# One mixer and the output projection of a diffusion block: where gates leave PSUM, which banks the decay loop uses, and when loads and read-backs are issued

## Chip, cores, metric

The kernel runs on one core of a Trainium2 chip, as one program in one launch. The metric is the device time of one execution in microseconds; a measurement is the median over several runs of the same kernel on the same chip. "PE" is TensorE, "PEld" its weight loads, "DVE" VectorE, "ACT" ScalarE, "POOL" GpSimd, "SP" the engine whose queue issues most of the transfers.

## The reference

One layer of a token mixer with three parallel head groups, a common output projection and an MLP, for 2048 latent and 256 context tokens, 1024 channels, in float32. Cut to what the change touches:

```python
(xa, ga, qb, kb, vb, gb, lr, qc, kc, vc, oc, i_fw, i_bw, f_fw, f_bw) = split_proj(h @ w_in)
# group B: gated linear attention in chunks of 64, 6 heads of 64, both directions d
la = heads(log_sigmoid(lr @ gla_w2[d] + gla_b2[d]) / 16)
b = cumsum(la, axis=chunk)            # decay inside a chunk
q_dec, k_dec = q * exp(b), k * exp(-b)
scores = where(causal, q_dec @ k_dec.T, 0)
u = (k * exp(b_last - b)).T @ v       # what a chunk adds to the state
s = exp(b_last) * s + u               # scan over the chunks, s_prev is s before
o = scores @ v + q_dec @ s_prev
# all groups
gate = concat(gelu(ga), silu(gb), sigmoid(oc))
y = head_rmsnorm(concat(yA, yB, yC), head_norm_g) * gate
x = x + g1 * (y @ w_out)
x = x + g2 * (relu(modulate(rmsnorm(x, norm2_g), sh2, sc2) @ w1) ** 2 @ w2)
return rmsnorm(x, final_g)
```

## The kernel before

The tokens lie in five groups (group 0 the 256 context tokens, groups 1 to 4 of 512 latent tokens). The stages follow each other in one long program: norm and modulation (to about 200 us), mixer A, the modulation of the MLP, mixer C (to about 800 us), mixer B (about 800 to 1250), the output projection (to 1480), the MLP (to the end).

Every matrix product of the projections is made of three float32 products with rounded operands, high by high, high by low and low by high (`products`, lines 357 to 371): for one block of 128 channels and one group that is 24 matmuls of 128x512 into one PSUM bank `acc`, after which `evac` takes the bank. Blocks of the input projection don't run in a stage of their own: `Filler` hands them out piecewise, so that they stand between the mixers' small matmuls. The order on PE is the order in which the program is written (a manual schedule). The other engines get their order from a scheduler, with priorities in a few places.

PSUM has eight banks here: three `pp` (block products), one `tr` (transposes, `trt`), and four of the mixer's own. In mixer B these four are one ring, `qk2`, from which the decay's pre-activation `xq`, the state products `u` and, in the second loop, the scores take their banks.

A gate block (`to_gate`, L489) turns a bank into GELU (blocks 0 and 1), SiLU (2 to 4) or sigmoid (5 to 7). It goes back and forth between ACT (square, absolute value, exponential, logarithm, exponential) and DVE (L497, L498 for GELU, L502 and L505), with the tile `t` and the bank itself as operands, and its bank is free only after the last product, L505. `evt` has three buffers.

Mixer B's first loop walks 30 steps (6 heads by 5 groups). `decay` loads the low-rank input on POOL's queue (`lr`, L1027), multiplies it into `xq`, computes log-sigmoid, the scan L1039 and the exponentials, and scales the keys `k` and queries `q`, which it stores. Three steps later `keys_t` transposes the keys into `trt()` and ACT copies them (`kt`, L1067). One step after that `chunk_u` multiplies them with the values into a bank `u`, and two DVE copies (L1077, L1079) take it to the state `U`; `chain` scans the state. Between these, `fil.share` runs gate blocks.

The second loop walks 24 steps (group, head pair, head). `scores` loads `q` and `k` (`qdD` and `kdD`, names `bk` and `bq`, four and three buffers) and pads `q` into `z` (L1147 on ACT, L1148 on DVE, three buffers), multiplies (L1155), and masks. `outputs`, two steps later, multiplies the scores with the values and the queries with the state (L1166, L1167). Between the two, `between_b` runs the remaining filler, then the loads of the output weights (`load_wo`), then the output projection as a generator, as far as the rows of y are ready.

The output projection works on 16 tiles of 128 tokens. `y_in` loads the gates `ga` and the mixers' output `yt`, squares it into `sq` (ACT, L1229), and scales it by its heads' norms (DVE, L1234). `y_t` transposes half a tile, multiplies it with the gates (L1249) and splits it into `yh` (ACT, L1250) and `yl` (POOL, L1251). `w_out` makes one half of 512 columns (24 matmuls, L1264 to L1266) and adds it to `x2` (DVE, L1269). `x_out` stores `x2`, normalises it into `xo` (L1278 squares it there, L1280 scales it) and stores that (L1281). Normalised tiles are read back (`xn`, L1343), transposed and modulated by `h2_tile` (L1312) for the first half of the MLP, among the products of later tiles. The pool of the projection has two `yt`, one `sq`, one `xo`, one `xn`.

## Time and profile before

| | |
|---|---|
| median of three runs | 2781.36 us (2778.57 to 2790.45) |
| the profiled execution | 2780.29 us, span 2778.5 us |
| PE busy | 2561.5 us, 92% of the span, 12239 instructions |
| PEld busy | 2081.4 us, 75% |
| DVE busy | 1754.9 us, 63% |
| ACT busy | 1161.4 us, 42% |
| POOL busy | 982.4 us, 35% |
| mean granted clock of PE | 0.965 |

Busy times are sums over one execution. An engine's idle time in a stretch is the stretch's length less its busy time there; the profile names for most of it the instruction that ended it. Register, branch, semaphore and DMA-issuing instructions don't count as busy. All lines are those of the kernel before.

### The profile page before, as it was taken

What the parts mean: (1) busy time and instruction counts of PE and PEld (TensorE: products, weight loads), DVE (VectorE), ACT (ScalarE), POOL (GpSimd) and SP (SyncE); (2) the same over time, 40 slices, a digit from 0 to 9 for tenths busy, and PEclk for the clock granted to TensorE, in tenths of its full rate; (3) what the DMA queues carried; (4) which work ended last, traced back from release to release, by engine and by line L of the source; (5) the groups of instructions that cost most, each with busy time, mean ns of one, the idle gap of its engine ahead of it and who ended that gap; (6) DMA issues with size and microseconds to landing.
All of it is one profiled execution on the core that took longest, in us unless ns stands there. A gap on an engine that the chain in (4) does not pass through costs nothing. (4 is left out here: it accounts for less than half of the span.)

```text
span 2778.5 us, 36372 instructions
## 1 busy us (share of the span) xinstructions
PE 2561.5 (92%) x12239; PEld 2081.4 (75%) x12239; DVE 1754.9 (63%) x3039; ACT 1161.4 (42%) x2053; POOL 982.4 (35%) x868
## 2 busy tenths in 40 slices
PE   5798889899999888888897999989999999999997
PEld 3676667788887676777776888867887888888876
DVE  7855476146646986656665787666666356545586
ACT  6755521133335666433334444544445332222343
POOL 5734411245444443334443343343432122222221
PEclk8999989999999999989998999999999999999999
DMA  7443355565656666766663777555554677656564
GB/s 221 143 138 110 95 159 163 155 159 157 156 153 174 183 177 187 242 192 203 233 204 104 205 211 223 171 183 163 144 156 139 221 244 242 211 176 202 169 210 152
DMA packets 490215, 495.24 MB, mean 178 GB/s; under 512 B 88226, under 2 KB 371580, under 8 KB 490028
## 3 DMA queue, kind: packets, MB, share of 16 engines
q1 hardware_dynamic: 464076, 465.58, 55.7%
q10 hardware_dynamic: 20480, 15.73, 1.7%
q0 software_dynamic: 5472, 11.60, 1.5%
q8 instruction: 97, 1.59, 0.2%
q14 instruction: 90, 0.74, 0.1%
HBM read 336.89 MB, written 155.92 MB: 177 GB/s over the span
## 5 line engine op out<-in xcount | busy, mean ns | idle before, releaser
L365 PE MATMUL pp<-hTh,whi 128*128 128x512 f32 (+1 forms) x1048 | 435.6, 416 | 14.5 <-DVE evt L505 10.9
L367 PE MATMUL pp<-hTh,wlo 128*128 128x512 f32 (+1 forms) x1048 | 410.4, 392 | 1.7 <-POOL wlo L313 1.3
L366 PE MATMUL pp<-hTl,whi 128*128 128x512 f32 (+1 forms) x1048 | 408.8, 390 | 0.2 <-DVE hTl L452 0.2
L1780 PE MATMUL yps<-bh,al 128*128 128x512 f32 x832 | 326.5, 392 | 3.8 <-POOL al L1405 2.4
L1778 PE MATMUL yps<-bh,ah 128*128 128x512 f32 x832 | 325.7, 392 | 0.0
L1779 PE MATMUL yps<-bl,ah 128*128 128x512 f32 x832 | 324.2, 390 | 0.0
L1405 POOL TENSOR_TENSOR al<-ar,ah 128x1024 fp32r<-128x1024 f32 x54 | 132.6, 2455 | 481.3 <-ACT ah L1642 470.8
L365 PEld LDWEIGHTS pp<-hTh,whi 128*128 128x128 f32 x1048 | 206.0, 197 | 52.0 <-DVE evt L505 12.7
L1642 ACT CAST ah<-ar 128x1024 fp32r<-128x1024 f32 x108 | 113.5, 1051 | 306.2 <-PE yps L1779 270.4
L367 PEld LDWEIGHTS pp<-hTh,wlo 128*128 128x128 f32 x1048 | 204.7, 195 | 45.6 <-POOL wlo L313 3.5
L366 PEld LDWEIGHTS pp<-hTl,whi 128*128 128x128 f32 x1048 | 205.6, 196 | 35.5 <-issue 1.9
L1780 PEld LDWEIGHTS yps<-bh,al 128*128 128x128 f32 x832 | 156.2, 188 | 42.9 <-POOL al L1405 4.3
L1779 PEld LDWEIGHTS yps<-bl,ah 128*128 128x128 f32 x832 | 156.3, 188 | 33.4
L1778 PEld LDWEIGHTS yps<-bh,ah 128*128 128x128 f32 x832 | 156.4, 188 | 31.9
L1408 POOL TENSOR_TENSOR uz<-tz 128x512 f32<-128x512 f32 x32 | 49.8, 1556 | 345.2 <-ACT whi L1413 176.2
L1478 PE MATMUL accy<-th,whi 128*128 128x512 f32 x384 | 152.6, 397 | 2.2 <-ACT th L1642 1.2
L1480 PE MATMUL accy<-th,wlo 128*128 128x512 f32 x384 | 150.7, 392 | 2.6 <-DVE wlo L1405 2.6
L1479 PE MATMUL accy<-tl,whi 128*128 128x512 f32 x384 | 151.0, 393 | 0.0
L1405 DVE TENSOR_TENSOR wlo<-wab,whi 128x512 fp32r<-128x512 f32 x124 | 115.2, 931 | 36.3 <-ACT whi L1413 36.3
L1405 DVE TENSOR_TENSOR wlo<-ws,whi 128x512 fp32r<-128x512 f32 x93 | 78.5, 845 | 81.8 <-ACT whi L1413 81.5
L1413 ACT CAST whi<-wab 128x512 fp32r<-128x512 f32 x124 | 76.7, 619 | 120.3 <-PE accy L1479 54.8
L1264 PE MATMUL pp<-woh,yh 128*128 128x512 f32 x256 | 106.2, 415 | 9.0 <-ACT yh L1250 9.0
(407 smaller groups left out, 6040.1 us busy)
## 6 DMA issues: line engine op xcount, KB each, us to landing
uD<-uz SPq DMA_DIRECT2D x224, 256.0 KB
ar<-uD SPq DMA_DIRECT2D x108, 512.0 KB
braw<-in_mlp_w_dram SPq DMA_DIRECT2D x84, 512.0 KB
wab<-in_mlp_w_dram SPq DMA_DIRECT2D x62, 512.0 KB
maw<-in_ada_w_dram SPq DMA_DIRECT2D x64, 256.0 KB
wraw<-in_w_in_dram SPq DMA_DIRECT2D x54, 256.0 KB
rb<-rD SPq DMA_DIRECT2D x96, 128.0 KB
aw<-in_ada_w_dram SPq DMA_DIRECT2D x32, 256.0 KB
```

What stands on the lines that cost most here:

```text
L365: nc.tensor.matmul(acc[:, 0:n], hi, hTh[g][:, k, :], start=k == 0, stop=False)
L366: nc.tensor.matmul(acc[:, 0:n], hi, hTl[g][:, k, :], start=False, stop=False)
L367: nc.tensor.matmul(acc[:, 0:n], lo, hTh[g][:, k, :], start=False, stop=k == KC - 1)
L1264: nc.tensor.matmul(acc, yh[:, k, :], woh[:, k, ns], start=k == 0, stop=False)
L1405: eng.tensor_tensor(o, a, b, op=ALU.subtract)
L1478: nc.tensor.matmul(acc, hi[:, k, :], T2[i][0][:, k, :], start=first and k == 0, stop=False, skip_group_check=True)
L1479: nc.tensor.matmul(acc, hi[:, k, :], T2[i][1][:, k, :], start=False, stop=False, skip_group_check=True)
L1480: nc.tensor.matmul(acc, lo[:, k, :], T2[i][0][:, k, :], start=False, stop=k == 3, skip_group_check=True)
L1642: nc.scalar.copy(hi, r_)
L1778: nc.tensor.matmul(acc, ah[:, p_, :], bh, start=p_ == 0, stop=False)
L1779: nc.tensor.matmul(acc, ah[:, p_, :], bl, start=False, stop=False)
L1780: nc.tensor.matmul(acc, al[:, p_, :], bh, start=False, stop=p_ == 7)
```

## The change

Five things are written in another way.

1. `to_gate`: DVE copies the bank to a tile `z` next to ACT's first reading of it, and all later operations of the gate read `z` or `t` from SBUF. The result goes into `e`.
2. Banks of the first loop: `keys_t` takes `trt()` and a bank of its own, `trk`, in turn; `xq` has two banks and `u` one, `uk`. The second loop opens its own pool with four banks `sc`.
3. `lr` is loaded one step ahead (`load_lr`), and 6 us of filler run ahead of the first step.
4. `load_qk` is split from `scores`: the loads of `q` and `k` and the padded copies of a step are written ahead of the scores of the step before.
5. Output projection: `xn` has two buffers and is read back a tile ahead; `y_in(i + 2)` stands ahead of the first half's products, `y_t(i + 1, nh)` ahead of the products `w_out(i, nh)`; the squares `sq` go into the buffer named `xo`, of which there is still one.

```diff
@@ -489,21 +489,25 @@
     def to_gate(b):
 
         def f(g, n, acc):
-            t, e = evt(), evt()
-            z = acc
+            e, z = evt(), evt()
             if b < 2:
-                z = t
+                t = evt()
                 nc.scalar.activation(t, acc, AF.Square)
+                nc.vector.tensor_copy(z, acc)
                 nc.vector.tensor_scalar(t, t, 2 * GELU_C * GELU_K, 2 * GELU_C, op0=ALU.mult, op1=ALU.add)
-                nc.vector.tensor_tensor(t, t, acc, op=ALU.mult)
-            nc.scalar.activation(e, z, AF.Abs)
+                nc.vector.tensor_tensor(t, t, z, op=ALU.mult)
+                nc.scalar.activation(e, t, AF.Abs)
+            else:
+                t = z
+                nc.scalar.activation(e, acc, AF.Abs)
+                nc.vector.tensor_copy(z, acc)
             nc.scalar.activation(e, e, AF.Exp, scale=-1.0)
             nc.scalar.activation(e, e, AF.Ln, bias=1.0)
-            nc.vector.scalar_tensor_tensor(t, z, 0.0, e, op0=ALU.min, op1=ALU.subtract)
-            nc.scalar.activation(t, t, AF.Exp)
+            nc.vector.scalar_tensor_tensor(e, t, 0.0, e, op0=ALU.min, op1=ALU.subtract)
+            nc.scalar.activation(e, e, AF.Exp)
             if b < 5:
-                nc.vector.tensor_tensor(t, t, acc, op=ALU.mult)
-            nc.sync.dma_start(gD[g][b], t)
+                nc.vector.tensor_tensor(e, e, z, op=ALU.mult)
+            nc.sync.dma_start(gD[g][b], e)
         return f
 
     for b in range(8):
@@ -996,7 +1000,8 @@
         nc.scalar.copy(w2s[0:64], w2v[0:64])
         nc.vector.tensor_tensor(w2s[64:96], w2v[64:96], w2h[64:96].bitcast(F32), op=ALU.subtract)
         st2.close()
-        pm = psum(st, "pmb")
+        stp = ExitStack()
+        pm = psum(stp, "pmb")
         bp = spool(st, "mxb")
         rst = bp.tile([P, 513], F32, name="rst")
         nc.sync.dma_start(rst, I["rst"])
@@ -1016,6 +1021,13 @@
 
         heads = {}
 
+        lrs = []
+
+        def load_lr(g):
+            lr = bp.tile([P, 512], F32R, name="lr", bufs=2)
+            nc.gpsimd.dma_start(lr[0:96, 0:GRP[g][1]], lrD[g])
+            lrs.append(lr)
+
         def decay(hh, g):
             p, hl = hh // 2, hh % 2
             if g == 0:
@@ -1024,9 +1036,8 @@
             A, B, U = heads[hh]
             t0, n = GRP[g]
             nch, c0 = n // P, t0 // P
-            lr = bp.tile([P, 512], F32R, name="lr", bufs=2)
-            nc.gpsimd.dma_start(lr[0:96, 0:n], lrD[g])
-            xq = pm.tile([P, 512], F32, name="qk2", bufs=4)
+            lr = lrs.pop(0)
+            xq = pm.tile([P, 512], F32, name="xq", bufs=2)
             nc.tensor.matmul(xq[:, 0:n], w2s[:, hh, :], lr[0:96, 0:n])
             bx, k = bp.tile([P, 2, 512], F32, name="bx", bufs=3), bt("bk", 4)
             la, pc = bx[:, 0, :], bx[:, 1, :]
@@ -1057,9 +1068,9 @@
             nc.sync.dma_start(v[:, 0:nch, :], vbD[g][:, 64 * hh:64 * hh + 64].rearrange("(t p) e -> p t e", p=P))
             return k, v
 
-        def keys_t(g, k):
+        def keys_t(i, g, k):
             n = GRP[g][1]
-            tp = trt()
+            tp = pm.tile([P, 512], F32, name="trk") if i % 2 else trt()
             for j in range(n // P):
                 nc.tensor.transpose(tp[:, j * P:(j + 1) * P], k[:, j * P:(j + 1) * P], ident)
             kt = bt("bkt")
@@ -1070,7 +1081,7 @@
         def chunk_u(hh, g, kt, v):
             U = heads[hh][2]
             nch, c0 = GRP[g][1] // P, GRP[g][0] // P
-            u = pm.tile([P, 512], F32, name="qk2", bufs=4)
+            u = pm.tile([P, 512], F32, name="uk", bufs=1)
             for j in range(nch):
                 nc.tensor.matmul(u[:, 64 * j:64 * j + 64], kt[:, j * P:(j + 1) * P], v[:, j, :])
             uv = u[:, 0:64 * nch].rearrange("p (c e) -> p c e", e=64)
@@ -1103,6 +1114,7 @@
 
         seq = [(hh, g) for hh in range(6) for g in range(5)]
         kv, kts = {}, {}
+        load_lr(seq[0][1])
         steps = iter(())
         AHEAD = 3
         LAST = len(seq) + AHEAD + 1
@@ -1111,11 +1123,15 @@
                 hh, g = seq[i]
                 if g == 0 and hh % 2 == 0:
                     fil.need(f"qb{hh // 2}")
+                if i == 0:
+                    fil.run(6.0)
+                if i + 1 < len(seq):
+                    load_lr(seq[i + 1][1])
                 kv[i] = decay(hh, g)
             next(steps, None)
             i2 = i - AHEAD
             if 0 <= i2 < len(seq):
-                kts[i2] = keys_t(seq[i2][1], kv[i2][0])
+                kts[i2] = keys_t(i2, seq[i2][1], kv[i2][0])
             fil.share(FB1, 2 * (LAST - i))
             i3 = i - AHEAD - 1
             if 0 <= i3:
@@ -1131,25 +1147,34 @@
             pass
 
 
+        stp.close()
+        pm = psum(st, "pmb2")
+        qks = {}
+
 
         qz = [bp.tile([P, 2, 512], F32, name="bx", bufs=3) for _ in range(3)]
         for t_ in qz:
             nc.gpsimd.memset(t_, 0.0)
 
-        def scores(i, p, g, hl):
+        def load_qk(i, p, g, hl):
             hh = 2 * p + hl
             q, k = bt("bk", 4), bt("bq", 3)
             nc.sync.dma_start(q, qdD[hh][g])
             nc.sync.dma_start(k, kdD[hh][g])
-            s = bp.tile([P, 4, 64], F32, name="bv", bufs=3)
-            nc.gpsimd.dma_start(s, sD[hh][:, 4 * g - 4:4 * g, :])
             z = qz[i % 3]
             nc.scalar.copy(z[0:64, 0, :], q[0:64, :])
             nc.vector.tensor_copy(z[64:128, 1, :], q[64:128, :])
+            qks[i] = q, k, z
+
+        def scores(i, p, g, hl):
+            hh = 2 * p + hl
+            q, k, z = qks.pop(i)
+            s = bp.tile([P, 4, 64], F32, name="bv", bufs=3)
+            nc.gpsimd.dma_start(s, sD[hh][:, 4 * g - 4:4 * g, :])
             w = bt("lr" if i % 2 else "bkt")
             wv = w.rearrange("p (c l) -> p c l", l=P)
             for jj in (0, 2):
-                sc = pm.tile([P, 2, 2, P], F32, name="qk2", bufs=4)
+                sc = pm.tile([P, 2, 2, P], F32, name="sc", bufs=4)
                 for j in range(2):
                     js = slice((jj + j) * P, (jj + j + 1) * P)
                     nc.tensor.matmul(sc[:, j, :, :], k[:, js], z[:, :, js])
@@ -1169,7 +1194,10 @@
         seq = [(p, g, hl) for g in LATG for p in range(3) for hl in range(2)]
         work = {}
         o = v = None
+        load_qk(0, *seq[0])
         for i in range(-2, len(seq)):
+            if i + 3 < len(seq):
+                load_qk(i + 3, *seq[i + 3])
             if i + 2 < len(seq):
                 work[i + 2] = scores(i + 2, *seq[i + 2])
             between(i)
@@ -1225,7 +1253,7 @@
             nc.sync.dma_start(ga[hf], gD[g][4 * hf:4 * hf + 4, :, j * P:(j + 1) * P].rearrange("b p t -> p b t"))
         yt = op_.tile([P, D], F32, name="yt", bufs=2)
         nc.sync.dma_start(yt, yD[g][j * P:(j + 1) * P, :])
-        sq = op_.tile([P, D], F32, name="sq", bufs=1)
+        sq = op_.tile([P, D], F32, name="xo", bufs=1)
         nc.scalar.activation(sq, yt, AF.Square)
         ss = op_.tile([P, 16], F32, name="hss", bufs=2)
         nc.vector.tensor_reduce(ss, sq.rearrange("p (h e) -> p h e", e=64), axis=AX.X, op=ALU.add)
@@ -1335,27 +1363,29 @@
             yield None
         for hf in range(2):
             y_t(0, hf)
-        built = 0
+        built, ahead = 0, None
         for i in range(16):
-            xn = None
-            if hp2 and built <= min(7, i - 2):
-                xn = wo["op"].tile([P, D], F32, name="xn", bufs=1)
-                nc.sync.dma_start(xn, xnD[built])
+            xn, ahead = ahead, None
+            if hp2 and built + (xn is not None) <= min(7, i - 1):
+                ahead = wo["op"].tile([P, D], F32, name="xn", bufs=2)
+                nc.sync.dma_start(ahead, xnD[built + (xn is not None)])
+            if i + 2 < 16:
+                yield from until(i + 2)
+                y_in(i + 2)
             for nh in range(2):
-                yield from w_out(i, nh)
-                if nh == 0 and i + 2 < 16:
-                    yield from until(i + 2)
-                    y_in(i + 2)
                 if i + 1 < 16:
                     y_t(i + 1, nh)
+                yield from w_out(i, nh)
                 if xn is not None:
                     h2_tile(wo["op"], tr2, built, nh, xn)
             if xn is not None:
                 built += 1
             x_out(i)
         for i in range(built, 8):
-            xn = wo["op"].tile([P, D], F32, name="xn", bufs=1)
-            nc.sync.dma_start(xn, xnD[i])
+            xn, ahead = ahead, None
+            if xn is None:
+                xn = wo["op"].tile([P, D], F32, name="xn", bufs=2)
+                nc.sync.dma_start(xn, xnD[i])
             for hf in range(2):
                 h2_tile(wo["op"], tr2, i, hf, xn)
 
```

The rows below are those of the program as built, in the order in which each engine takes them, with the semaphores that a row waits for. The first place is DVE in the decay loop, around the end of one `decay` and of one SiLU gate: L1041 reads what POOL subtracted (`bB`), L1043 to L1047 finish the decay and scale the keys, L502 and L505 belong to the gate (`pp` is its bank), L1077 copies the state product. Before:

```order
1238 L1041 COPY bB<-bx 128x4 [waits Pool_49]
1239 L1043 TENSOR_TENSOR bx<-bx,bB 128x512 [waits DVE_49]
1240 L1044 COPY bA<-bx 128x4 [waits DVE_49]
1241 L1045 TENSOR_TENSOR bA<-bA,bx 64x4 [waits DVE_49]
1242 L502 SCALAR_TENSOR_TENSOR evt<-pp,evt 128x512 [waits Activation_49]
1243 L1047 TENSOR_TENSOR bk<-bk,bx 128x512 [waits DMAHW3_49,DMAHW1_49,Activation_49]
1244 L505 TENSOR_TENSOR evt<-evt,pp 128x512 [waits Activation_49]
1245 L1077 COPY bU<-qk_9498 64x256 [waits PE_49]
```

And of the change, where the scan is L1050, the copy out of the gate's bank L503, and L1041 has become L1052, L502 L506, L505 L509, L1077 L1088:

```order
1270 L1049 SCALAR_TENSOR_TENSOR bx<-xq,bx 128x512 [waits Activation_49]
1271 L1050 SCALAR_TENSOR_TENSOR bx<-rst,bx 128x512 [waits DVE_49]
1272 L503 COPY evt<-pp 128x512 [waits Activation_49]
1273 L1052 COPY bB<-bx 128x4 [waits Pool_49]
1274 L1054 TENSOR_TENSOR bx<-bx,bB 128x512 [waits DVE_49]
1275 L1055 COPY bA<-bx 128x4 [waits DVE_49]
1276 L1056 TENSOR_TENSOR bA<-bA,bx 64x4 [waits DVE_49]
1277 L506 SCALAR_TENSOR_TENSOR evt<-evt 128x512 [waits DMAHW1_49,Activation_49]
1278 L1058 TENSOR_TENSOR bk<-bk,bx 128x512 [waits DMAHW6_49,DMAHW2_49,Activation_49]
1279 L509 TENSOR_TENSOR evt<-evt 128x512 [waits Activation_49]
1280 L1088 COPY bU<-uk 64x256 [waits PE_49]
1281 L1090 COPY bU<-uk 64x256
```

The gate's two later operations no longer name `pp`; a copy that does stands between the scan and the row that waits for POOL; the state copies read the one bank `uk`.

The second place is ACT in the output projection, around the square of `yt` (L1229 before, L1257 after), the cast to `yh` (L1250, then L1278), and the square of `x2` (L1278 before, L1306 after; L215 and L216 are the norms' logarithm and exponential, L1298 and L1326 a modulation of `h2_tile`). Before:

```order
1130 L1229 ACTIVATE sq<-yt 128x1024 [waits DMAHW2_49]
1131 L215 ACTIVATE hnr<-hss,epsc 128x16 [waits DVE_49]
1132 L216 ACTIVATE hnr<-hnr 128x16 [waits Activation_49]
1133 L1250 CAST yh<-yg 128x512 [waits DVE_49,Pool_49]
1134 L1298 ACTIVATE tr_12065<-tr_12514,mT_3004,sc_3005 128x128 [waits DVE_49,PE_49]
1135 L1278 ACTIVATE xo,s_12569<-x_12449 128x1024 [waits DMAHW6_49,DMAHW5_49,DVE_49]
```

And of the change:

```order
1128 L216 ACTIVATE n2r<-n2r 128x1 [waits Activation_49]
1129 L1257 ACTIVATE xo<-yt 128x1024 [waits DMAHW1_49,DMAHW0_49,DVE_49]
1130 L1326 ACTIVATE tr_12141<-tr_12674,mT_3004,sc_3005 128x128 [waits DVE_49,PE_49]
1131 L1278 CAST yh<-yg 128x512 [waits DVE_49]
1132 L215 ACTIVATE hnr<-hss,epsc 128x16 [waits DVE_49]
1133 L216 ACTIVATE hnr<-hnr 128x16 [waits Activation_49]
1134 L1306 ACTIVATE xo,s_12729<-x_12641 128x1024 [waits DVE_49]
```

The square of `yt` now writes `xo` and waits for two transfers and for DVE, where it waited for one transfer; the wait for the transfers that free `xo` has moved to it from the square of `x2`, and the row of DVE's that scales the tile before into `xo` lies ahead of it too.

The third place is PE in the output projection: L1247 transposes `yt` and L1312 `xn` before, L1275 and L1340 after; L1264 and L1266 are the first and the last product of a step over the channels, L1292 and L1294 after. Before:

```order
4608 L1266 MATMUL pp<-woh,yl 128x512
4609 L1247 MATMUL tr_12639<-ident,yt 128x128 [waits DMAHW2_49,DVE_49,PE_49]
4610 L1247 MATMUL tr_12639<-ident,yt 128x128 x3
4611 L1312 MATMUL tr_12648<-ident,xn 128x128 [waits DMAHW5_49]
4612 L1312 MATMUL tr_12648<-ident,xn 128x128 x3
4613 L1264 MATMUL pp<-woh,yh 128x512
```

And of the change:

```order
4615 L1294 MATMUL pp<-woh,yl 128x512
4616 L1340 MATMUL tr_12718<-ident,xn 128x128 [waits DVE_49]
4617 L1340 MATMUL tr_12718<-ident,xn 128x128 x3
4618 L1275 MATMUL tr_12766<-ident,yt 128x128 [waits DMAHW1_49,DVE_49,Activation_49]
4619 L1275 MATMUL tr_12766<-ident,yt 128x128 x3
4620 L1292 MATMUL pp<-woh,yh 128x512 [waits Activation_49]
```

The transposes of `xn` come first and wait for no transfer at this place; those of `yt` stand right ahead of the next products, half a tile earlier than before.

## Rows read from the trace of the kernel before

**Rows 1.** Busy time by stretch: start:end and length in us, then each engine.

```profile
core 0: us, PE busy (x) PEld busy (x) DVE busy (x) ACT busy (x) POOL busy (x), PEclk, DMA share, GB/s
880.00:1047.00 167.00, 144.68 (x691) 117.19 (x689) 144.76 (x289) 109.11 (x207) 71.38 (x63) 0.96 0.61 176
1047.00:1110.00 63.00, 54.21 (x250) 43.36 (x251) 43.13 (x89) 38.68 (x71) 23.88 (x22) 0.95 0.65 191
1110.00:1250.00 140.00, 118.67 (x635) 104.56 (x633) 83.39 (x155) 56.66 (x118) 46.83 (x52) 0.89 0.68 215
1250.00:1420.00 170.00, 152.78 (x749) 124.51 (x748) 112.07 (x218) 59.57 (x130) 74.43 (x54) 0.97 0.67 219
1420.00:1480.00 60.00, 51.99 (x227) 40.34 (x225) 28.53 (x52) 15.89 (x36) 22.71 (x16) 0.96 0.49 159
```

**Rows 2.** PE's waits, 800 to 1110: total us, times, longest us.

```profile
PE tr L1064 <- ACT bkt L1067: 18.9, 11, 3.8
PE pp L365 <- DVE evt L505: 10.9, 6, 2.7
```

**Rows 3.** ACT's and DVE's waits, 880 to 1047.

```profile
ACT evt L503 <- DVE evt L502: 25.8, 14, 3.9
...
DVE bB L1041 <- POOL bx L1040: 8.8, 9, 1.5
```

**Rows 4.** DVE's groups by shape, 880 to 1047: busy us, mean ns; idle before.

```profile
L505 DVE TENSOR_TENSOR evt<-evt,pp 128x512 f32<-128x512 f32 x20 | 13.6, 682 | 1.6 <-ACT evt L503 1.4
L1047 DVE TENSOR_TENSOR bk<-bk,bx 128x512 f32<-128x512 f32 x15 | 12.3, 821 | 2.0 <-DMA bk<-kbD 0.9 <-ACT bx L1046 0.9
...
L502 DVE SCALAR_TENSOR_TENSOR evt<-evt 128x512 f32<-128x512 f32 x8 | 8.4, 1045 | 0.3 <-ACT evt L501 0.2
L502 DVE SCALAR_TENSOR_TENSOR evt<-pp,evt 128x512 f32<-128x512 f32 x12 | 8.3, 688 | 2.8 <-ACT evt L501 2.6
```

**Rows 5.** The tile `ayo` of mixer A: minimum, median, maximum ns.

```profile
L620 DVE COPY ayo<-tr x8: 672/686/692, 241.0 to 329.9; 128x512 f32<-128x512 f32 x8
```

**Rows 6.** Timeline of the decay loop: start us, duration us.

```profile
924.47 1.00 PE L1075 MATMUL qk<-bv,bkt 128*128 128x64 f32 x8
...
926.77 0.43 DVE L1079 COPY bU<-qk 64x256 f32<-64x256 f32 x1
```

**Rows 7.** Timeline of the scores loop; in brackets the wait ahead.

```profile
1152.63 0.39 PE L1167 MATMUL tr<-bv,bk 128*128 128x64 f32 x2
...
1153.05 0.32 SPq L1142 DMA_DIRECT2D bk<-qd  x1
...
1155.72 1.17 DVE L1148 COPY bx<-bk 64x512 f32<-64x512 f32 x1 [0.77 <-DMA bk<-qd]
...
1157.14 1.97 PE L1155 MATMUL qk<-bx,bq 128*128 128x256 f32 x8 [0.61 <-DVE bx L1148]
```

**Rows 8.** PE's waits, 1250 to 1480.

```profile
PE tr L1312 <- DMA xn<-xn: 11.1, 7, 2.4
PE pp L1266 <- POOL yl L1251: 5.5, 8, 1.5
```

**Rows 9.** SP's issues in the projection, 1253 to 1262.

```profile
1254.89 0.32 SPq L1281 DMA_DIRECT2D xn<-xo  x1
...
1259.21 0.32 SPq L1343 DMA_DIRECT2D xn<-xn  x1
```

**Rows 10.** Timeline of one tile of the projection, 1349 to 1365.

```profile
1349.71 0.69 DVE L1269 TENSOR_TENSOR x<-x,pp 128x512 f32<-128x512 f32 x1 [1.79 <-PE pp L1266]
...
1354.56 0.32 SPq L1281 DMA_DIRECT2D xn<-xo  x1
1355.79 1.06 ACT L1229 ACTIVATE sq<-yt 128x1024 f32<-128x1024 f32 x1 [2.57 <-DMA yt<-yD]
...
1358.30 0.66 PE L1312 MATMUL tr<-ident,xn 128*128 128x128 f32 x4 [1.75 <-DMA xn<-xn]
...
1360.81 2.05 DVE L1234 TENSOR_TENSOR yt<-yt,hnr 128x1024 f32<-128x1024 f32 x1
...
1364.57 0.69 DVE L1269 TENSOR_TENSOR x<-x,pp 128x512 f32<-128x512 f32 x1 [1.72 <-PE pp L1266]
```

## The prediction

> **What bounds the kernel now.** I read the stage windows first. TensorE (PE) is busy nearly everywhere, so only a stretch in which it idles can give time back. Of what the change touches there are four [rows 1]: the decay loop with the gates of the GELU and SiLU blocks (880 to 1047 us), its end with sigmoid gates (to 1110), the scores loop (to 1250), the output projection (to 1480). PE idles 167.0 - 144.7 = 22.3, 8.8, 21.3, and 17.2 + 8.0 = 25.2 us in them, 78 us together. That is all there is to win, 2.8%.
>
> Next the list of PE's waits. In the decay loop PE waits 18.9 us for ScalarE's copy of the one key-transpose bank and 10.9 us for a projection bank whose gate is still being computed [rows 2]. These are the two waits that the change aims at. But the reader should ask what makes those two late: ScalarE waits for VectorE (DVE), 25.8 us at one line of the gates alone [rows 3], and DVE is busy 144.8 of the 167.0 us, exactly as long as PE [rows 1]. PE's waits are the visible end of a queue on DVE.
>
> **The change part by part.** The sum is made against the profiled execution, 2780.3 us (span 2778.5); the median of the three runs, 2781.4, lies 1 us above it.
>
> *Gates, 880 to 1047 us.* ScalarE's count stays. DVE gets one copy from PSUM per gate. The trace of before has such a copy of 128x512, 0.686 us [rows 5], and 20 gates finish here (their last product stands 20 times [rows 4]): 13.7 us. Also the inputs of the other operations move from PSUM to SBUF. The form with PSUM takes 0.682 us (product) and 0.688 (min and subtract); the forms with SBUF alone take 0.821 and 1.045 in the same stretch [rows 4]. That adds 20 x 0.139 = 2.8 for the last product, 8 x 0.139 = 1.1 for the inner product of the eight GELU gates, 12 x 0.357 = 4.3 for the others' subtraction: 8.2 us. DVE's work goes from 144.8 to 166.7 us, all of the 167.0 that the stretch lasts now. With no penalty for SBUF it would be 158.5.
> The Trainium skill speaks against this edit: SBUF — State Buffer, section "Who interferes with whom", says that a VectorE instruction with two SBUF inputs contends with a GpSimd instruction that reads SBUF, and one with at most one SBUF input does not. The rows agree in size (0.69 against 0.82 and 1.05); by that rule alone, were GpSimd silent, 13.7 us would be added, and by the rows 21.9.
> What is left of DVE's idle time decides. It is 22.2 us now; 8.8 of these wait for GpSimd's subtraction [rows 3], and the new order puts a gate's copy just there, between the scan and the wait (first place of the order above), so I count that part as filled. The waits on ScalarE shrink as DVE falls behind; I keep 5 us. The stretch becomes 166.7 + 5 = 171.7: **+5 us**. From below, 158.5 with no idle (-8.5); from above, 166.7 and all 22.2 of idle (+22).
> PE's two waits go, but PE then waits for DVE at another place: the products for the state now have one bank, and its two copies are DVE's. Now the products at 924.47 us run while the preceding pair of copies ends only at 927.20 [rows 6]; with one bank PE would stand there 2.7 us. That adds nothing to DVE's work; it is where the stall shows next.
>
> *Sigmoid gates, 1047 to 1110 us.* About eight gates at 0.686 + 0.357 = 1.04 us bring DVE from 43.1 to 51.4 us; PE has 54.2 of 63 [rows 1]. Here DVE has room, so PE can win back up to 8.8; the single state bank takes some. **-4 us** (0 to -9). The earlier loads of the low-rank input cost nothing and give nothing: no wait of PE for them appears beside those in [rows 2]; if their cover were gone, each would cost its few us of transfer.
>
> *Scores loop, 1110 to 1250 us.* "One step ahead" is a statement about the program, so I looked at what the load waits for. The query tiles have four buffers, before and after. PE ends the output products that read the old tile (the last listed starts at 1152.63), SP issues the load at 1153.05, DVE's padded copy starts at 1155.72 when it has landed, and PE's scores begin at 1157.14 [rows 7]. The load already leaves in the moment its buffer comes free, and the buffer comes free at the same matmul as before. What can be won is the place of the padded copies in the queues of ScalarE and DVE (they no longer stand behind the other work of a step) and of the other loads on SP: **-2 us**. Bounds: -12 if about half of the 21.3 us of idle goes, +4 if copies that wait for a transfer hold up the emptying of score banks behind them.
>
> *Output projection, 1250 to 1480 us.* Read-back one tile ahead with two buffers takes away 11.1 us of waits, transposes ahead of the matmuls most of the 5.5 us for `yl` [rows 8]. But to make room the squares of the next `yt` now go into the buffer `xo`, of which there is one. Its square on ScalarE must wait till the normalised tile in it has been stored. Chain, from the moment DVE adds the last product of a tile (1349.71): store issued at 1354.56, +4.85 [rows 10]; a store of this size is read back, which must wait for it, 4.32 us after its issue (1254.89 to 1259.21) [rows 9], so +9.2; from the start of the square to the end of the scaling of `yt`, 1355.79 to 1362.86, is 7.07 [rows 10], so +16.2. At that point PE may transpose that `yt`, and the change wants it one half tile earlier than before. A tile takes 14.86 us now (1349.71 to 1364.57) with one wait of 1.75 [rows 10], so 13.1 without. From that transpose PE needs 12.7 us to the end of the second tile on (13.1 less one group of transposes, 0.66 from its first start to its last end [rows 10]; it overlaps its neighbours, and I take 0.4), so two tiles take 16.2 + 12.7 = 28.9, one 14.5. I take -0.4 for some 12 tiles, **-5 us**. Bounds: -21 with no wait left (1.75 x 12), +11 if a 256 KB transfer of 2.7 us [rows 7] stands ahead of each store (+1.35 less 0.4 per tile).
>
> **Sum:** +5 - 4 - 2 - 5 = -6, so 2774 us. The waits that the change names disappear, and others take most of their time. About 0.5%, 14 us, is what a measurement of this kernel can tell from no change.
>
> **Rivals.**
> *The waits go and little replaces them.* PE idles 78 us in the stretches, and if DVE fills its gaps (-8), the sigmoid part gives its 9, the scores 6 and the projection 12 (half its bound and a little), the kernel is at 2780 - 35 = 2745. For it: each wait in [rows 2, 8] has a direct remedy. Against: DVE's floor of 158.5 and the chain through `xo`. Chance 0.34, spread from 2735 to 2767.
> *DVE overflows* (the other side). The stretch from 880 is bound by DVE; with its penalty for SBUF inputs and the idle that it has today it takes 188.9 us, +22; with the sigmoid part at 0, scores at 0 and the projection at -3 that is +19, 2799. It ends beyond 0.5% once DVE keeps about 17 of its 22.2 us of idle. For it: DVE runs its operations strictly in order and each gate still goes DVE, ScalarE, DVE. Against: the copies stand in the gaps. Chance 0.16, with the projection's +11 in it.
> *The change does nothing where it says "ahead"* (loads bound by buffers, DVE level): the terms for scores and low-rank loads are 0, and the total 2776 stays inside the forecast's case.
>
> **How the numbers follow.** The forecast's case has 0.50; its own range, from the smaller swings of each term, is 2767 to 2795. That is "within 0.5%". Faster by more has 0.34, slower by more 0.16. To hold 8 in 10 the range reaches well into the faster rival and to the centre of the slower: 2744 to 2798.
>
> **What the changed profile would show.** Right: PE no longer waits for the last gate product or, but for a little, for the key copy; in their place waits of PE for the copies out of the state bank, and DVE busy at 93% or more between about 880 and 1050. The SBUF forms in the gates take clearly more than 0.7 us on average. In the scores loop DVE and ScalarE still wait for the query loads by about as much. In the projection the waits for the read-back are gone, and in their place PE waits for the scaled `yt`, with ScalarE idle before its square until the store lands; a tile still takes over 14 us. Wrong: tiles of 13.1 us (the store lands early, or its wait is hidden), or a gate stretch under 160 us (DVE packs better than I count); both would put the kernel near 2745. A gate stretch over 185 us would put it near 2799.

## The result

The changed kernel takes 2808.3 us (median of 6 runs, 2799.3 to 2811.0) against 2780.9 for the kernel before: ratio 1.0082, 95% interval 1.0056 to 1.0108. The forecast was 2774, between 2744 and 2798; the kernel became slower, and lies above the upper end. The profiled execution has a span of 2809.2 us.

To see where, I cut both profiles at the same places of the program: the end of mixer C, the last copy of a state product, the second addition to `x2` of the first tile, the last such addition. Before, then after (columns as in [rows 1]):

```profile
802.30:1112.70 310.40, 277.09 (x1314) 225.21 (x1313) 225.97 (x455) 178.25 (x331) 125.64 (x117) 0.97 0.63 181
1112.70:1250.10 137.40, 116.07 (x620) 102.29 (x618) 82.97 (x154) 56.02 (x117) 46.67 (x52) 0.89 0.69 217
1250.10:1476.90 226.80, 204.58 (x972) 164.66 (x971) 139.20 (x264) 73.15 (x159) 97.15 (x70) 0.97 0.63 204
```

```profile
807.90:1127.90 320.00, 284.52 (x1314) 232.74 (x1313) 247.96 (x484) 178.94 (x331) 130.13 (x117) 0.93 0.60 175
1127.90:1269.10 141.20, 118.85 (x624) 104.76 (x622) 86.48 (x160) 56.71 (x118) 47.27 (x53) 0.87 0.70 217
1269.10:1508.40 239.30, 207.86 (x967) 170.60 (x966) 163.89 (x264) 70.61 (x158) 89.01 (x69) 0.94 0.57 190
```

Decay loop +9.6 us, scores +3.8, projection +12.5. The 5.6 us ahead of them are in code that is the same (mixer C ends between 799.0 and 807.9 in the profiles of the kernels below), and what follows is as long as before.

**Decay loop.** The two waits of [rows 2] are gone. In their place stand waits of PE for the one state bank `uk`, 33.7 us against the 29.8 that went, and in longer pieces:

```profile
PE uk L1086 <- DVE bU L1090: 6.9, 6, 1.6
PE uk L1086 <- DMA qd<-bq: 6.5, 1, 6.5
PE uk L1086 <- DVE bA L1056: 6.4, 2, 4.4
PE uk L1086 <- issue: 5.8, 1, 5.8
```

The names behind the arrow are only what ended nearest; the place itself tells more. In the timeline DVE comes to the copies out of `uk` (L1088, L1090) after a step of the chain that took 1.31 us (L1110, 0.28 mostly; it meets a POOL operation), and PE, whose last matmul ended 6.53 us earlier, goes on:

```profile
918.01 1.26 POOL L1064 TENSOR_TENSOR bq<-bq,bx 128x512 f32<-128x512 f32 x1
918.04 1.31 DVE L1110 SCALAR_TENSOR_TENSOR bU<-bU,bW 128x64 f32<-128x64 f32 x1
...
920.46 0.42 DVE L1088 COPY bU<-uk 64x256 f32<-64x256 f32 x1
920.89 0.43 DVE L1090 COPY bU<-uk 64x256 f32<-64x256 f32 x1
...
921.58 1.94 PE L1086 MATMUL uk<-bv,bkt 128*128 128x64 f32 x8 [6.53 <-DMA qd<-bq]
```

PE's idle time in the loop is 320.0 - 284.5 = 35.5 us, before 33.3. What grew is PE's busy time for the same 1314 matmuls, by 7.4 us, and the windows around this wait show why (PEclk is the third number from the end):

```profile
914.00:916.00 2.00, 1.05 (x5) 0.53 (x3) 1.94 (x7) 0.39 (x1) 0.00 (x0) 1.00 1.10 331
916.00:918.00 2.00, 0.00 (x0) 0.00 (x0) 1.38 (x4) 1.94 (x4) 1.02 (x1) 0.88 0.44 145
918.00:920.00 2.00, 0.00 (x0) 0.00 (x0) 2.00 (x7) 0.27 (x1) 1.76 (x2) 0.50 0.34 131
920.00:922.00 2.00, 0.42 (x2) 0.45 (x3) 1.89 (x7) 1.14 (x3) 0.00 (x0) 0.50 0.93 239
922.00:924.00 2.00, 2.00 (x10) 1.90 (x10) 1.95 (x8) 1.92 (x4) 0.00 (x0) 0.50 0.77 190
924.00:926.00 2.00, 2.00 (x7) 1.52 (x6) 1.94 (x5) 1.46 (x4) 0.93 (x1) 0.50 0.54 184
926.00:928.00 2.00, 2.00 (x7) 1.57 (x6) 1.99 (x4) 1.74 (x3) 1.35 (x1) 0.56 0.23 79
928.00:930.00 2.00, 2.00 (x12) 1.68 (x11) 1.95 (x4) 0.00 (x0) 0.25 (x1) 1.00 0.70 149
```

The granted clock falls from 2.4 to 1.2 GHz while PE waits, and in the windows behind the wait it stays there for some 5 us of work.

**Gates.** The copies cost what was forecast; the SBUF forms cost next to nothing in all (before, L502 took 14.4 + 8.4 us for 29, L505 13.6 for 20):

```profile
L506 DVE SCALAR_TENSOR_TENSOR evt<-evt 128x512 f32<-128x512 f32 x29 | 23.1, 797 | 1.8 <-ACT evt L505 1.6
L503 DVE COPY evt<-pp 128x512 f32<-128x512 f32 x21 | 14.3, 681 | 2.6 <-ACT evt L502 2.4
L509 DVE TENSOR_TENSOR evt<-evt 128x512 f32<-128x512 f32 x20 | 13.9, 695 | 1.0 <-ACT evt L507 0.8
```

The mean of L506 hides two kinds: 26 of the 29 take at most 0.69 us, three take 1.2 to 2.3. Each of the three began while a POOL operation was running, and ended 0.55 us after it:

```profile
976.50 2.76 POOL L1111 TENSOR_TENSOR bU<-bU,bW 128x1024 f32<-128x1024 f32 x1 [0.16 <-DVE bU L1110]
977.47 2.33 DVE L506 SCALAR_TENSOR_TENSOR evt<-evt 128x512 f32<-128x512 f32 x1
```

**Projection.** PE no longer waits for the read-back [rows 8], but for `yt`:

```profile
PE tr L1275 <- issue: 19.9, 7, 4.3
PE tr L1275 <- DVE yt L1262: 10.8, 3, 5.9
```

Two tiles in the timeline (rows of DVE, ACT, SP and PE by start):

```profile
1413.80 0.60 PE L1340 MATMUL tr<-ident,xn 128*128 128x128 f32 x4
...
1417.34 1.23 DVE L1262 TENSOR_TENSOR yt<-yt,hnr 128x1024 f32<-128x1024 f32 x1
1418.48 0.68 DVE L1297 TENSOR_TENSOR x<-x,pp 128x512 f32<-128x512 f32 x1
1418.67 0.63 PE L1275 MATMUL tr<-ident,yt 128*128 128x128 f32 x4 [4.27 <-issue]
...
1419.20 1.06 ACT L1306 ACTIVATE xo<-x 128x1024 f32<-128x1024 f32 x1 [5.46 <-DVE x L1297]
...
1424.96 0.32 SPq L1309 DMA_DIRECT2D xn<-xo  x1
...
1426.23 0.60 PE L1340 MATMUL tr<-ident,xn 128*128 128x128 f32 x4
...
1427.94 1.06 ACT L1257 ACTIVATE xo<-yt 128x1024 f32<-128x1024 f32 x1 [6.11 <-issue]
...
1432.62 0.60 PE L1340 MATMUL tr<-ident,xn 128*128 128x128 f32 x4
...
1433.88 1.23 DVE L1262 TENSOR_TENSOR yt<-yt,hnr 128x1024 f32<-128x1024 f32 x1
...
1435.02 0.68 DVE L1297 TENSOR_TENSOR x<-x,pp 128x512 f32<-128x512 f32 x1
1435.20 0.63 PE L1275 MATMUL tr<-ident,yt 128*128 128x128 f32 x4 [1.98 <-issue]
...
1441.50 0.32 SPq L1309 DMA_DIRECT2D xn<-xo  x1
...
1446.08 1.06 ACT L1257 ACTIVATE xo<-yt 128x1024 f32<-128x1024 f32 x1 [7.71 <-DVE yg L1277]
...
1451.62 1.23 DVE L1262 TENSOR_TENSOR yt<-yt,hnr 128x1024 f32<-128x1024 f32 x1
1452.77 0.68 DVE L1297 TENSOR_TENSOR x<-x,pp 128x512 f32<-128x512 f32 x1
```

Read it as a chain: addition 1418.48, square 1419.20, store of `xo` 1424.96, square of the next `yt` into the same `xo` 1427.94, scaling to 1435.11, then PE's transposes, and on DVE the next tile's addition, 16.5 us after the first; the second tile goes the same way and takes 17.75. Two things in it were not in the forecast. The addition stands behind the scaling in DVE's order: PE had done that tile's products by 1413.80, DVE took the addition at 1418.48. And behind a wait PE is slow: from the transposes at 1418.67 to the next ones 7.56 us (to 1426.23), without a wait ahead 5.95 (1426.67 to 1432.62).

### The profile page after: what moved, and what is told of

It is laid out like the page before. It is cut to its first block, busy times and chain, and to the rows that moved or that the text cites. A ratio compares the mean times of both kernels' runs of the same rounds, so it can differ in the third digit from the quotient of the medians.

```text
span 2809.2 us, 36438 instructions
## 1 busy us (share of the span) xinstructions
PE 2571.9 (92%) x12239; PEld 2095.5 (75%) x12239; DVE 1807.3 (64%) x3071; ACT 1160.2 (41%) x2053; POOL 983.5 (35%) x868
## 5 line engine op out<-in xcount | busy, mean ns | idle before, releaser
L1809 PEld LDWEIGHTS yps<-bl,ah 128*128 128x128 f32 x832 | 156.3, 188 | 33.7
L313 POOL TENSOR_TENSOR wlo<-wraw,whi 128x512 fp32r<-128x512 f32 x54 | 74.8, 1384 | 120.4 <-ACT whi L312 109.2
```

The source lines that it names most:

```text
L1809: nc.tensor.matmul(acc, ah[:, p_, :], bl, start=False, stop=False)
```

## The experiments

All times are medians; ratios are to the kernel before on the same chip, with their 95% interval. Stage lengths are cut as above, from one profile each.

**The projection.** *Squares in `xo`*, on the kernel before:

```diff
-        sq = op_.tile([P, D], F32, name="sq", bufs=1)
+        sq = op_.tile([P, D], F32, name="xo", bufs=1)
```

> The kernel before with one edit of the projection alone: the squares of yt go into the buffer xo. Theory (the loop through xo hurts only together with the new order, in which yt is wanted half a tile earlier and DVE scales yt ahead of the last addition of the tile before): the store of xo leaves at 1354.56 in the trace of before and the square starts at 1355.79, so the square is late by about 2 us, which the half tile hides: 2781, within 6 us of before. Rival (sharing xo costs the tiles 1.6 us each in any order): 2798. PE's waits for the read-back stay at about 11 us by both.

2793.7 us, 1.0042 (1.0027 to 1.0057), projection 236.9 us. Neither figure: sharing the buffer costs 12 us in the old order too, so the half tile does not hide it. From the fourth tile on DVE takes the addition right behind the scaling here too.

*The whole projection part on the kernel before* (that line and the last hunk of the diff, of which the core):

```diff
+                ahead = wo["op"].tile([P, D], F32, name="xn", bufs=2)
...
+                if i + 1 < 16:
+                    y_t(i + 1, nh)
+                yield from w_out(i, nh)
```

> The kernel before with the whole projection part of the change and nothing else. Theory (the loop last addition, square, scaling and store of xo, square and scaling of the next yt closes once per tile, 16.5 us in the changed kernel against 14.9 before): tiles of about 16.5 us, 12 to 17 us more than before, 2793 to 2798. Rival (the projection is late only because what comes from the mixer is late): tiles of 14.9 or less, 2770 to 2781.

2792.9 us, 1.0043 (1.0027 to 1.0059), projection 236.1 us. The part is slow by itself, at the lower edge of what the chain was to cost.

*The chain cut in the changed kernel*, in two ways: a full buffer for the squares and one `xn`; or four steps through a small one, and two `xn`.

```diff
-        sq = op_.tile([P, D], F32, name="xo", bufs=1)
+        sq = op_.tile([P, D], F32, name="sq", bufs=1)
-                ahead = wo["op"].tile([P, D], F32, name="xn", bufs=2)
+                ahead = wo["op"].tile([P, D], F32, name="xn", bufs=1)
...
```

> The changed kernel with the squares in a buffer of their own again, paid for with one buffer xn in place of two. Theory (loop through xo): the loop is cut, the waits for the read-back come back (about 11 us), tiles of 14 to 15 us, 2786 to 2794 where the changed kernel has 2808. Rival (the new order of transposes, or the clock, makes the tiles long): tiles stay above 16 us, 2803 to 2810.

```diff
-        sq = op_.tile([P, D], F32, name="xo", bufs=1)
-        nc.scalar.activation(sq, yt, AF.Square)
+        for r in range(4):
+            sq = op_.tile([P, 256], F32, name="sq", bufs=1)
+            nc.scalar.activation(sq, yt[:, 256 * r:256 * r + 256], AF.Square)
+            nc.vector.tensor_reduce(ss[:, 4 * r:4 * r + 4], ...)
```

> The changed kernel with the squares in a small buffer of their own of 256 columns, in four steps, and two buffers xn as in the change. Theory (loop through xo): neither the loop nor the read-back holds PE, tiles near 13.5 us, 25 to 35 us less than the changed kernel, 2773 to 2783. Rival (order or clock): tiles above 16 us, 2803 to 2812, with the four steps costing ACT and DVE a little.

2783.9 us, 1.0001 (0.9990 to 1.0012), and 2773.7 us, 0.9962 (0.9948 to 0.9975). Both are the theory's side, the first 2 us below its range: with one `xn` PE waits 5.5 us for the read-back, not 11. The second one's projection:

```profile
1263.70:1471.70 208.00, 195.60 (x952) 161.08 (x950) 141.99 (x301) 75.17 (x194) 89.98 (x69) 0.98 0.66 218
```

31 us less than in the changed kernel, with four squares and four sums in place of one. *The same on the kernel before*, with nothing else of the change:

> The kernel before with the projection part of the change, but the squares in a small buffer of their own of 256 columns in four steps. Theory (reading back a tile ahead and transposing ahead is worth the waits that it takes away, once the loop through xo is cut): projection 208 us against 227 before, 2761 to 2766. Rival (the gain shown with the rest of the change came from the mixer's delay, which leaves the projection less to wait for): 2770 to 2780.

2760.8 us, 0.9919 (0.9898 to 0.9939), projection 210.3 us. Reading back and transposing ahead, with the squares in four steps, gain 0.8%; the shared buffer alone turned that into a loss of 0.4%.

**How the chain closes.** *The addition ahead of the scaling*, in the changed kernel (the lines that make the dependency; norm scale and scaling are also written behind the products of the tile before):

```diff
+        one = wo["op"].tile([P, 1], F32, name="one", bufs=2)
+        nc.vector.tensor_scalar(one, x2[:, D - 1:D], 0.0, 1.0, op0=ALU.mult, op1=ALU.add)
+        nc.vector.scalar_tensor_tensor(rs, rs, one, r1, op0=ALU.mult, op1=ALU.mult)
```

> The changed kernel, in which the scaling of yt is made to depend on the last addition of the tile before (a column of x2 times 0 plus 1 enters the scale), so that DVE takes the addition first. Squares stay in xo. Theory (the loop closes once per tile because the addition stands behind the scaling in DVE's queue): the loop is open, but PE now waits about 2.3 us for addition, scale and scaling in each tile, tiles of 15 to 15.5 us in place of 16.5, 2788 to 2798. Rival (the loop through xo has its 16.5 us whatever the order of these two, as sharing xo alone makes it): tiles of 16.5 or more, 2806 to 2820.

2818.0 us, 1.0128 (1.0110 to 1.0146), tiles of 17.0 us. PE waits 2.5 us in each tile, as expected, but the tile gets no shorter. The time is the rival's, but not for its reason. The chain is not what holds the tile here: DVE is idle until PE is done (first row). What was left out is the clock behind each wait, here in the rows of one (7.54 us to the next transposes) and in the windows behind another, which ended at 1403.15:

```profile
1417.28 0.69 DVE L1312 TENSOR_TENSOR x<-x,pp 128x512 f32<-128x512 f32 x1 [0.81 <-PE pp L1309]
...
1420.17 0.63 PE L1290 MATMUL tr<-ident,yt 128*128 128x128 f32 x4 [2.49 <-issue]
1427.71 0.60 PE L1355 MATMUL tr<-ident,xn 128*128 128x128 f32 x4
```

```profile
1403.00:1405.00 2.00, 1.85 (x9) 1.65 (x10) 1.41 (x4) 0.61 (x3) 1.27 (x1) 0.83 0.93 348
1405.00:1407.00 2.00, 2.00 (x6) 1.54 (x6) 1.87 (x4) 0.21 (x1) 1.19 (x2) 0.50 0.68 231
1407.00:1409.00 2.00, 2.00 (x9) 1.60 (x8) 0.66 (x1) 0.00 (x0) 1.81 (x2) 0.81 0.25 104
```

*The chain 1.06 us longer*, alone and then with the changed kernel's order of DVE held by a dependency:

```diff
         nc.scalar.activation(sq, yt, AF.Square)
+        nc.scalar.activation(sq, yt, AF.Square)
```

> The changed kernel with the square of yt taken twice into xo, 1.06 us more in the loop; ACT has room for it. Theory (loop closed once per tile): each of about 13 tiles is 1 us longer, 2817 to 2824 where the changed kernel has 2808. Rival (the loop spans two tiles, and something else makes the tiles 16.5 us): 0 to 0.5 us per tile, 2806 to 2814.

2799.6 us, 1.0065 (1.0047 to 1.0082): no longer than the changed kernel. But the scheduler answered the longer chain by putting the addition ahead of the scaling in every third tile, so this tells nothing of the order.

```diff
+            one = wo["op"].tile([P, 1], F32, name="one", bufs=2)
+            nc.vector.tensor_scalar(one, yts[i + 2][0][:, D - 1:D], 0.0, 1.0, op0=ALU.mult, op1=ALU.add)
+            nc.vector.scalar_tensor_tensor(x2[:, ns], x2[:, ns], one, acc, op0=ALU.mult, op1=ALU.add)
```

> The changed kernel with the square of yt taken twice into xo (1.06 us more in the chain), and with the last addition of a tile made to depend on the scaling of the yt two tiles on, so that DVE's order stays that of the changed kernel in every tile (with the square twice alone, the scheduler moved the addition ahead in every third tile). Theory (with this order the chain closes once per tile): tiles of 17.5 to 18 us against 16.5, 2818 to 2828. Rival (the chain spans two tiles): 0 to 0.5 us per tile, 2806 to 2814.

2817.7 us, 1.0134 (1.0113 to 1.0154). Between the first and the fourteenth last addition 17.07 us per tile (1265.93 to 1487.90), in the changed kernel 16.49 (1269.08 to 1483.47): 0.58 per tile, half of what was added. By this figure neither theory is shown: a chain over two tiles would give 0.53, one closed in each tile 1.06. The total lies just under the first theory's range.

The starts in the two traces, tile by tile, settle it. In the changed kernel, in the ten tiles from 1319.35 to 1483.47 (16.4 us each), DVE takes every addition as the scaling ends, with no idle time ahead of it, and in nine of them ACT has been idle for 5.0 to 7.7 us ahead of the square: the chain closes once in each tile. In this version the dependency closes it once as well, and it grows by less than was added because other parts of it got shorter: in the same ten tiles the store leaves 5.1 us after the addition in place of 5.9, and from the end of the squares to the next addition it is 5.5 in place of 6.0.

**The decay loop.** *Gates alone* (the first hunk of the diff) and *banks alone* (also the second loop's own pool), on the kernel before:

```diff
+                nc.vector.tensor_copy(z, acc)
-                nc.vector.tensor_tensor(t, t, acc, op=ALU.mult)
+                nc.vector.tensor_tensor(e, e, z, op=ALU.mult)
```

> The kernel before with the gates of the change alone (copy out of the bank, later operations from SBUF). Theory (DVE sets the pace of the decay loop, and the copies and SBUF forms load it by 19 us there, as the changed kernel's windows show): PE's wait for the last gate product, 10.9 us, goes, its wait for the key copy grows by about as much, 2781 to 2793. Rival (the copy only frees banks, DVE packs it): 2768 to 2775.

```diff
+            tp = pm.tile([P, 512], F32, name="trk") if i % 2 else trt()
+            xq = pm.tile([P, 512], F32, name="xq", bufs=2)
+            u = pm.tile([P, 512], F32, name="uk", bufs=1)
```

> The kernel before with the banks of the change alone: a second bank for key transposes, two for xq, one for the state products. Theory (one state bank is emptied by two DVE copies that stand in DVE's queue, PE waits long at it, and the granted clock falls to 1.2 GHz after the longest waits): the key copy's 18.9 us go, 15 to 30 us of waits at the state products come, 2781 to 2792. Rival (the state bank is late only because the gate copies load DVE): waits there under 8 us, 2768 to 2775.

2790.6 us, 1.0031 (1.0020 to 1.0043), and 2782.6 us, 0.9998 (0.9985 to 1.0011). The loop of each:

```profile
802.80:1122.70 319.90, 283.70 (x1314) 231.15 (x1313) 241.19 (x484) 178.80 (x331) 131.24 (x117) 0.94 0.61 176
```

```profile
803.60:1115.30 311.70, 282.64 (x1314) 232.56 (x1313) 225.89 (x456) 178.47 (x331) 125.57 (x117) 0.94 0.63 180
```

Both times are those of the first theory. The gates alone make the loop 9.5 us longer: PE's wait for the last gate product goes, that for the key copy grows from 18.9 to 24.2 us, with a longest of 5.2, and PE's busy time grows by 6.6. A GELU gate now also holds all three `evt` buffers, before two of them; what that costs was not tried apart. With the banks alone PE idles 29.1 us, 4 less than before, and all of that and more is lost again in the clock (PE busy +5.6). PE waits 27.7 us at `uk` without any gate copy: the single bank is late by its own place in DVE's queue.

*Two banks for `uk` and one for `xq`*, and *the gates as before* (the first hunk undone), both on the changed kernel with the chain cut in four steps (2773.7):

```diff
-            xq = pm.tile([P, 512], F32, name="xq", bufs=2)
+            xq = pm.tile([P, 512], F32, name="xq", bufs=1)
-            u = pm.tile([P, 512], F32, name="uk", bufs=1)
+            u = pm.tile([P, 512], F32, name="uk", bufs=2)
```

> The changed kernel with the squares in a buffer of their own in four steps (2773.7 as measured), and in the decay loop two banks for the state products and one for xq in place of one and two. Theory (the single state bank is the stall of the decay loop): PE's 33 us of waits at the state products fall under 12, the clock there stays at 0.96 or more, 2755 to 2766. Rival (DVE's queue is the bound, banks only move the wait): PE waits for xq's one bank or for gate banks by as much, 2770 to 2778.

> The changed kernel with the squares in a buffer of their own in four steps (2773.7 as measured), and the gates as they were before, from the bank and without a copy. Theory (the gate copies load DVE by 19 us in the decay loop and so make the single state bank late): PE's waits at the state products fall to 15 us or less, its wait for the last gate product comes back at about 10, 2762 to 2770. Rival (the single state bank is late by its own order in DVE's queue): waits at the state products stay near 30, and the gate banks add theirs, 2774 to 2785.

2776.2 us, 0.9977 (0.9963 to 0.9992), PE now waiting 40.7 us for `xq`; and 2775.4 us, 0.9972 (0.9961 to 0.9983), still 29.8 us at `uk`. Both rivals: moving the scarce bank moves the wait, and on top of the single bank the copies cost little more (loop 318.5 us without them, 320.0 with).

*One ring of three banks for `xq` and `u`, and a second key bank*, with the projection of 2760.8 us:

```diff
-            tp = trt()
+            tp = pm.tile([P, 512], F32, name="trk") if i % 2 else trt()
-            xq = pm.tile([P, 512], F32, name="qk2", bufs=4)
+            xq = pm.tile([P, 512], F32, name="qk2", bufs=3)
...
-            u = pm.tile([P, 512], F32, name="qk2", bufs=4)
+            u = pm.tile([P, 512], F32, name="qk2", bufs=3)
```

> The same projection, and in the decay loop a second bank for key transposes with one ring of three banks for xq and the state products in place of the ring of four; gates, loads and scores as before. Theory (the key copy's wait goes and a ring leaves the state products two banks more often than the fixed split does, so no long waits arise): PE's waits in the decay loop under 20 us with the clock at 0.97, 2748 to 2758. Rival (with DVE late, any bank that is taken away shows as a wait elsewhere): waits of 28 us or more there, 2760 to 2768.

2757.7 us, 0.9904 (0.9881 to 0.9926), the lowest time of all, though its interval overlaps that of the projection alone (0.9898 to 0.9939).

```profile
807.20:1115.10 307.90, 277.42 (x1316) 223.35 (x1315) 225.89 (x456) 177.75 (x331) 126.20 (x117) 0.98 0.64 181
```

PE idles 30.5 us there, about as long as with the fixed split and as long as the rival said, but in no wait over 2.7 us, and the clock stays at 0.98. *The scores' loads on top of it*:

> The kernel with the projection part (squares in four steps in their own buffer), a second bank for key transposes and a ring of three banks (2757.7, 0.9904 of before), and the scores' loads and padded copies one step ahead. Theory (that edit alone gave 0.9986, within what can be told): 0.988 to 0.991. Rival (next to other banks it costs, as the banks did with the low-rank loads): 0.993 to 0.996.

2759.3 us, 0.9919 (0.9899 to 0.9940): nothing, within what can be told. The decay loop takes 307.6 us here and 307.9 above, with the ring; 311.7 in both versions that have the fixed split and the low-rank loads as before.

**Loads ahead.** The scores' loads alone, and the low-rank loads with the 6 us of filler alone, on the kernel before:

```diff
+            if i + 3 < len(seq):
+                load_qk(i + 3, *seq[i + 3])
```

> The kernel before with the loads and padded copies of the scores loop written one step ahead, and nothing else. Theory (the load leaves when the last product that reads its buffer has run, so writing it earlier changes nothing but places in queues): scores loop 137 us as before within 4, 2778 to 2786. Rival (padded copies that wait for a transfer hold up what is behind them on ACT and DVE): scores loop above 142 us, 2787 or more. Other rival (the loads do go earlier): about 128 us, 2772.

```diff
+                if i == 0:
+                    fil.run(6.0)
+                if i + 1 < len(seq):
+                    load_lr(seq[i + 1][1])
```

> The kernel before with the low-rank loads one step ahead and 6 us of filler ahead of the first step, and nothing else. Between the end of mixer C and the last state copy the kernel before takes 310 us, with the banks alone 312, with all but the gate copies 318. Theory (the remaining 6 us come from this edit, which shifts what stands where in the loop): 315 to 318 us there, 2785 to 2790. Rival (the edit is nothing and the 6 us are the variation of one execution): 309 to 313, 2780 to 2784.

2781.6 us, 0.9986 (0.9970 to 1.0001), and 2787.1 us, 1.0008 (0.9990 to 1.0027). The scores loop takes 133.0 us in the first; the decay loop 313.1 in the second, where five kernels with the loop of before have 310.4 or 310.5. Then banks with either of the two, with the projection of 2760.8 us (0.9919):

> The kernel before with the projection part (squares in four steps in a buffer of their own, 2760.8 as measured, 0.9919 of before), the banks of the change, and the low-rank loads and filler of the change. Alone the banks gave 0.9998 and the loads 1.0008. Theory A (banks and loads are harmless apart and cost some 10 us together, since the kernel with these, the scores' loads and no gate copies has 0.9972): 0.995 to 0.998, 2768 to 2776. Theory B (they add up, the cost comes with the scores' loads): 0.991 to 0.994, 2759 to 2765.

> The same with the banks and the scores' loads ahead, and low-rank loads and filler as before. Theory A (the cost is that of banks with low-rank loads): 0.990 to 0.993, 2756 to 2763. Theory B (the cost comes with the scores' loads next to the banks): 0.995 to 0.998, 2768 to 2776, with the scores loop above 140 us.

2770.5 us, 0.9952 (0.9934 to 0.9969), loop 318.6 us; and 2763.1 us, 0.9937 (0.9922 to 0.9952), loop 311.7, scores loop 135.0. By the totals the two can't be told apart, and the second lies between its theories. By the loops it is the low-rank loads and the filler that cost next to the single bank, 6.9 us; by the profile again in the clock, 285.5 us of PE's busy time with 0.93 in the first. Which of the loads and the filler it is was not tried apart.

## Why the prediction was wrong

**Output projection, -5 forecast, +12.5 measured: the step that failed.** The mechanism was named (square waits for the store, +16.2 us from the addition to the scaled `yt`), and the chain is as long as that: 1418.48 to 1435.11 is 16.6. It is the cause: with the squares in a buffer of their own the whole kernel gains 1.2%, with (1.0082 to 0.9962) or without (1.0043 to 0.9919) the rest of the change. Wrong was the step "so two tiles take 16.2 + 12.7 = 28.9, one 14.5", which closes the chain over two tiles, through PE's products. In the changed kernel two tiles take 34.3 (1418.48 to 1452.77), because the chain closes in each of them, on DVE: the addition stands behind the scaling, though PE was done with the products 3.6 us before (at 1449.13 for the addition at 1452.77). So a tile takes the chain's own length, 16.4 us on average. The 16.2 of the forecast was nearly the time of one tile. DVE's order shows in the rows of the program ahead of any run; I had followed ACT's order and PE's, not DVE's. The clock is a second bound close by: opened at the addition, the tiles grow to 17.0 us, as PE works at 1.2 GHz behind its waits (0.50 in the windows shown).

**Gates, +5 and -4 forecast, +9.6 measured for the loop.** DVE's copies were sized well (29 by 0.68 us). The SBUF forms were mis-sized: I took the 1.045 us of eight GELU subtractions for the price of the form, +8.2 us with the rest. Five of those eight took 0.67 to 0.69 us and three 1.5 to 1.8. All 29 take 0.797 on average after and 0.786 before, and the last product 0.695 against 0.682. The Trainium skill's rule on two SBUF inputs (SBUF — State Buffer, "Who interferes with whom") agrees with the trace, one operation at a time: the three long ones before and the three after each began while a POOL operation on SBUF was running, and ended 0.55 us after it. None of the DVE operations of 128x512 that read a bank was long (at most 0.69 us). So the form costs only where it meets POOL, and that was three times before and three times after (five times with the gates alone).

DVE's order, which I counted as filling gaps, does not bind by its sum: DVE is busy 248 of 320 us, and 151 of the 170 from 880 to 1050, 89% where I expected 93 or more. What costs is that PE's waits, with nearly the same sum (35.5 us idle against 33.3), are longer pieces (6.5, 5.8 and 4.4 us, before at most 3.8 [rows 2]), and that the clock falls behind them: 7.4 of the 9.6 us are PE's busy time. That term was not in the sum at all.

**The state bank** as the next stall was right in place. Its 15 waits are 2.2 us each on average, near the 2.7 of [rows 6], but single ones reach 6.5, and the stretch from 880 had no term for them.

**Scores loop, -2 forecast:** +3.8 in the profile, nothing alone (0.9986). The loads are waited for as before, as said: ACT and DVE idle 28.3 us for them, before 30.2. Kernels that leave this loop unchanged have 134 to 139 us in it, those with only its own pool of four banks 130 to 133, those with the loads ahead 130 to 143; what decides was not tried apart. **Low-rank loads, 0 forecast:** nothing alone by the total (2.7 us of loop in one profile), 6.9 us of loop next to the single bank.

**Sum.** By the ratios the change loses 0.82%, 23 us: the chain through `xo` took 34, the projection's gain without it is 22, and gates, banks and loads lose the other 12 or so (0.9962 against 0.9919). Alone these give 8, 0, 2 and -4; that they give more together is not clear of the intervals. In the decay loop they don't add up: 9.5, 1.3, 2.7 and 0.1 us alone, 9.6 together. The overflow rival had the right sign and the wrong place.

## What to carry to other kernels

A buffer that is lent to a second use joins two chains: walk the chain to where it meets itself, in the order of every engine on it, DVE's as well, before counting a period. Read the single durations behind a mean before making it the price of a form. Count PE's long waits, not only their sum: many short ones (28, none over 2.7 us) cost less than a few long ones. Three banks in one ring did better in the decay loop than the same three in a fixed split (308 us against 312); in the whole time this is not clear of the noise.

## What the runs showed of the hardware

That a wait costs more than its length. In the projection the same 720 matmuls of 128x512, with nearly the same small ones (952 to 972 records in all), keep PE busy for 195.6 us where it idles 12.4, 204.6 where it idles 22.2, 207.9 where it idles 31.4, and 213.6 where it idles 35.3 (the kernel with the addition first). A wait of 1.75 us [rows 10] left the clock at 1.00; behind one of 1.98 it was 0.50 from 1437 to 1439, and the next half tile took 7.56 us (1435.20 to 1442.76), as behind one of 4.27. The kernel before behind its 1.75 us, and then the whole projection of the kernel with the addition first:

```profile
1359.00:1361.00 2.00, 2.00 (x10) 1.63 (x9) 2.00 (x10) 0.63 (x2) 0.53 (x1) 1.00 0.73 274
```

```profile
1260.95:1509.90 248.95, 213.63 (x968) 174.18 (x966) 142.30 (x280) 73.91 (x158) 90.36 (x69) 0.92 0.56 182
```

And that DVE waits for POOL one operation at a time. In the decay loop of the changed kernel the long ones among the scans (L1050 over 512 columns, 7 of 24 take 2.1 to 2.3 us, in the median 1.23), the steps of the state chain (L1110, 17 of 81 take 0.46 to 1.39, in the median 0.28) and the gates' subtractions (L506, three of 29) all met a POOL operation, and ended a fixed time after it: 1.08, 0.08 and 0.55 us. The 24 of L1049, 21 of L503 and 8 of L496, which read a bank, never took more than 0.69 us.
